# Gate and up projections of a SwiGLU layer: seven half-size products in place of eight, with the layer's input kept whole in DRAM

## The chip, the cores and the metric

The kernel runs on one core of one Trainium2 chip. The metric is device microseconds of the whole program, the median of three runs. Names used below: PE is TensorE (matmuls), PEld its weight loads, DVE VectorE, ACT ScalarE, POOL GpSimd, SP SyncE, whose queue issues most of the loads.

## The reference, cut to what matters

One layer of a diffusion trunk: a mixer (a gated delta rule in both directions beside a Fourier mixing), an output projection, and a SwiGLU feed-forward layer with a final norm. 2176 tokens (128 of a prompt, 2048 of a sample), 1024 channels, 2816 hidden columns. The change is in the feed-forward layer:

```
h2   = rmsnorm(x1, g_ffn) * (1 + scale2) + shift2      # x1: after the mixer's residual
g, u = split(h2 @ w_gu, 2)                             # [2176,1024] x [1024, 2*2816], float32
y    = x1 + gate2 * ((silu(g) * u) @ w_down)
out  = rmsnorm(y, g_final)
```

## The kernel before, in words

Activations lie transposed, channels on the partitions: 1024 channels are KT = 8 blocks of 128, and tokens run along the free axis. Float32 products are made of three matmuls: every operand is split into a high part (ACT, a copy that rounds to 12 bits) and a low part (DVE, the operand minus its high part), and PE adds high·high, high·low and low·high in PSUM. The high and low parts carry the letters h and l at the end of their names (wh, wl; ah, al; dh, dl).

The program has phases: the input projection, the inverses and the scans, then `outputs` (output projection and second norm of each tile of 128 tokens, beside the scans), then `phase_d`, the feed-forward layer, which starts near 1307 us of a span of 2889 us.

`out_norm` writes each tile's normalised input to DRAM in its two parts (`h2_d[0]` on ACT's queue, `h2_d[1]` on POOL's).

`phase_d` takes three blocks of tokens (768, 768 and 640), in the order in which `outputs` finishes their tiles, so the last tiles belong to the last block. For each block:

1. It loads the block's high and low parts (`h2`, L1173, on SP).
2. **Gate and up.** For each of FT = 22 column tiles j, and for gate then up: the weights of 128 columns, 1024 rows (`w_gu`, 512 KB, L1184, into the three slots of the pool "st"), are split into wh and wl (128x1024 each, two buffers each); for each half of the tokens (384 or 320) PE runs 8 k-blocks x 3 matmuls into one PSUM bank: 2 x 2 x 24 = 96 matmuls a tile. ACT puts Silu(gate) into `a`, DVE multiplies the up projection into it. All 22 `a` tiles stay in SBUF.
3. **Down.** For each half of the 1024 output columns: for each of the 22 k, split `a[k]` into ah, al and 512 weight columns (`w_dn`, L1222) into dh, dl, and run 3 matmuls for each tile of 128 tokens, into one bank a tile. Then for each tile the epilogue: `gy` = bank x gate2 (DVE), load of the residual from DRAM (`x_f`, L1246; two pieces in the second half), the sum (DVE), its squares (ACT). In half 0 the sum times g_final goes back to DRAM (L1252). In half 1 three small POOL instructions make `rstd`, ACT scales one piece and DVE the other, and POOL issues both writes of y (L1262).

`ah`, `al`, `dh`, `dl`, `gy` (6 buffers), `g2` (2) and `x_f` (4) have buffers of their own in the pool `dp`.

The order of instructions on each engine is not that of the code: a scheduler that simulates the engines sets it when the program is built, and each engine then runs its list in order. SP's list holds the loads of all steps, so a load that waits for a buffer holds back every later load. The helpers record all arithmetic at one line each (L117 matmul, L123 tensor_tensor, L133 activation).

Of the kernel before, what the change touches and what calls it, by code (L numbers as in the profile page):

```python
# [36 lines left out]

CONSTS = {}
# [47 lines left out]
class K:  # L86
# [51 lines left out]
    def split(self, hi, lo, src, eng=None, copy=None):  # L138
        """src = hi + lo, both with 12 significant bits."""
# [6 lines left out]
    def rsqrt(self, out, x):  # L146
        """out = x ** -0.5 for a few values per partition."""
# [25 lines left out]
    def psum(self, *banks):  # L173
        """PSUM's eight banks as rings of so many under the tags m, acc and tr."""
# [5 lines left out]
    def setup(self):  # L180
# [38 lines left out]
        self.h2_d = d([2, P, KT, N], F32, name="h2_d")  # L219
# [29 lines left out]
    def ada_tiles(self):  # L249
        """Places for a block of rows of w_ada in two parts and, for two blocks at a time, as it comes."""  # L250
# [6 lines left out]
    def mod_columns(self, which, *source):  # L257
        """The scale and shift of norm `which` (0: mix, 1: ffn) by channel: x -> x * a + b."""
# [7 lines left out]
    def load_split(self, hi, lo, src, width, raw_p, tag, *engs):  # L266
        """Rows of a weight (128 by width) into its two parts."""
# [4 lines left out]
    def norm(self, x, which, work):  # L272
        """rmsnorm of a tile of 128 tokens, and a place for its transpose."""
        h = work.tile([P, KT, P], F32, tag="h", name="h", bufs=2 - which)
# [7 lines left out]
    def norm_T(self, xn, h, which, r, hi, lo):  # L282
        """The transpose of a normalised tile, modulated, in two parts."""
        for g in range(2):
# [11 lines left out]
            ks = slice(g * 4, g * 4 + 4)  # L296
            self.split(hi[:, ks], lo[:, ks], h[:, ks])

# [44 lines left out]
    def phase_a(self, wk):  # L343
        """The normalised and modulated activations, transposed; the gates' inputs and f, by token."""
# [244 lines left out]
    def decays(self, work, c0, m):  # L589
        """exp of the difference of a chunk's cumulative decays, where it counts, for both pairs and directions."""  # L590
# [17 lines left out]
    def pair_products(self, work, n, c0, m, kq, dT, q, ssk):  # L608
        """For a pair of heads: decayed products of keys with keys and with queries; the keys by token."""
# [34 lines left out]
    def scales(self, work, c0, m, st, ssk):  # L644
        """Per token: strength / |k|^2 and strength / |k| (for the inverses), -decay / |k|."""
# [14 lines left out]
    def rows_of(self, pool, cols, dst):  # L660
        """The columns of `cols` to rows of DRAM."""
# [650 lines left out]
```

## Time and profile before

| | us |
|---|---|
| median of three runs (2886.11 to 2893.64) | 2887.48 |
| the profiled execution's span | 2888.6 |
| PE busy in it (95%) | 2731.7 |
| PEld busy (86%) | 2490.9 |
| DVE busy (51%) | 1470.7 |
| ACT busy (42%) | 1201.4 |
| POOL busy (12%) | 358.3 |

The profile is of one execution; its span is 1.1 us above the median. Busy time is the union of an engine's instructions; matmuls overlap one another, so the duration of one is longer than the distance to the next, and the rate is read from counts in a window or from the distance between starts. In a timeline row the bracket at the end says how long the engine stood idle before the instruction and what released it. PEclk is the granted clock as a share of full speed (1.00 is 2.4 GHz, half of it 1.2 GHz).

### The profile page before, as it was taken

The page shows a single profiled execution, that of the slowest core. Times are in us where ns is not written, and L with a number is a line of the kernel's source. Part 1 is how long each engine was busy: PE and PEld are TensorE (multiplying, and loading weights), DVE is VectorE, ACT ScalarE, POOL GpSimd, SP SyncE. Part 2 cuts the span into 40 slices and gives each one's busy share as a digit, 9 for nine tenths or more (in the row PEclk, how much of TensorE's full clock was granted, in tenths as well). Part 3 has the DMA queues.
Part 4 walks back from the last instruction along what each step waited for, and adds up shares of the span by engine and source line. Part 5 has one row for each costly group of instructions (what it writes and reads, how often), then busy time and mean ns, then how long its engine had stood idle before and what let it go on. Part 6 is the DMA issues. An engine that isn't in the chain of part 4 may idle for free.

```text
span 2888.6 us, 43615 instructions
## 1 busy us (share of the span) xinstructions
PE 2731.7 (95%) x16561; PEld 2490.9 (86%) x16561; DVE 1470.7 (51%) x2772; ACT 1201.4 (42%) x2587; POOL 358.3 (12%) x503
## 2 busy tenths in 40 slices
PE   7999788899899899998999999999999999999998
PEld 4888687788788778878999978899999789999986
DVE  6345698998997677762222225432222354222354
ACT  8755454332478778752111123321111333112243
POOL 1213244331200022210000000010000001000000
PEclk9999899899999999999999999999999999999999
DMA  9937775545456667674222243342122434322123
GB/s 322 293 121 210 194 219 168 162 154 184 138 179 200 197 198 221 214 211 147 66 60 65 66 128 115 101 139 66 59 66 65 118 110 158 93 79 74 59 94 133
DMA packets 440462, 407.54 MB, mean 141 GB/s; under 512 B 97932, under 2 KB 362556, under 8 KB 439356
## 3 DMA queue, kind: packets, MB, share of 16 engines
q1 hardware_dynamic: 349740, 308.77, 35.0%
q0 software_dynamic: 16384, 55.85, 5.7%
q10 hardware_dynamic: 74128, 40.13, 5.0%
q8 instruction: 131, 2.15, 0.3%
q14 instruction: 79, 0.65, 0.1%
HBM read 301.42 MB, written 103.25 MB: 140 GB/s over the span
## 4 chain that ended last, share of the span: by engine, by line
PE 38%; issue 13%; DMA 2%; SPq 1%; ACT 0%; DVE 0%; POOL 0%; POOLq 0%; ACTq 0%; DVEq 0%
PE m L117 19%; PE acc L117 19%; SPq L1173 1%; DMA x_f<-x_d 1%; DMA w_dn<-w_down 0%; DMA h_d<-h2h 0%; DMA h<-h_d 0%; DMA y<-x_f 0%; POOL rstd L123 0%; ACT gy L133 0%; DMA x_d<-x_f 0%; DVE x_f L123 0%; POOL rstd L127 0%; DVE gy L123 0%; ACT x_f L133 0%
## 5 line engine op out<-in xcount | busy, mean ns | idle before, releaser
L117 PE MATMUL acc<-h,wh 128*128 128x384 f32 (+1 forms) x2112 | 515.4, 327 | 2.3 <-DMA h<-h_d 2.3
L117 PE MATMUL m<-h,wh 128*128 128x384 f32 (+1 forms) x2112 | 512.4, 326 | 0.0
L133 ACT ACTIVATE wh<-w_gu 128x1024 fp32r<-128x1024 f32 x132 | 139.9, 1060 | 573.4 <-PE m L117 377.1
L117 PEld LDWEIGHTS acc<-h,wh 128*128 128x128 f32 x2112 | 373.9, 189 | 2.9 <-issue 2.6
L117 PEld LDWEIGHTS m<-h,wh 128*128 128x128 f32 x2112 | 371.9, 188 | 0.0
L123 DVE TENSOR_TENSOR wl<-w_gu,wh 128x1024 fp32r<-128x1024 f32 x132 | 161.7, 1225 | 396.1 <-ACT wh L133 396.1
L117 PE MATMUL acc<-hb,w_in 128*128 128x258 f32 (+1 forms) x2304 | 329.2, 299 | 19.2 <-DMA hb<-hT 13.7
L117 PE MATMUL acc<-h,wl 128*128 128x384 f32 (+1 forms) x1056 | 345.2, 327 | 0.4 <-DVE wl L123 0.4
L117 PE MATMUL m<-h,wl 128*128 128x384 f32 (+1 forms) x1056 | 344.1, 326 | 0.3 <-DVE wl L123 0.3
L117 PEld LDWEIGHTS acc<-hb,w_in 128*128 128x128 f32 x2304 | 314.0, 196 | 29.7 <-issue 13.1
L123 DVE TENSOR_TENSOR a<-a,m 128x384 f32<-128x384 f32 (+1 forms) x132 | 69.9, 531 | 347.1 <-PE m L117 347.1
L123 DVE TENSOR_TENSOR al<-a,ah 128x768 fp32r<-128x768 f32 (+1 forms) x128 | 117.2, 916 | 247.3 <-ACT ah L133 247.2
L133 ACT ACTIVATE ah<-a 128x768 fp32r<-128x768 f32 (+1 forms) x128 | 104.0, 813 | 301.3 <-PE acc L117 227.6
L117 PEld LDWEIGHTS acc<-h,wl 128*128 128x128 f32 x1056 | 199.2, 189 | 0.8 <-DVE wl L123 0.7
L117 PEld LDWEIGHTS m<-h,wl 128*128 128x128 f32 x1056 | 198.2, 188 | 0.6 <-DVE wl L123 0.6
L1252 POOL DMA_DIRECT2D x_d<-x_f x17 | 9.2, 541 | 1280.7 <-DVE x_f L123 1280.4
L117 PE MATMUL m<-dh,ah 128*128 128x512 f32 x384 | 151.2, 394 | 8.3 <-ACT dh L133 8.3
L117 PE MATMUL m<-dl,ah 128*128 128x512 f32 x384 | 150.2, 391 | 0.6 <-DVE dl L123 0.6
L117 PE MATMUL m<-dh,al 128*128 128x512 f32 x384 | 149.7, 390 | 0.0
L130 DVE SCALAR_TENSOR_TENSOR y<-conv_in,wconv,y 128x256 f32<-128x256 f32 (+1 forms) x216 | 126.2, 598 | 40.9 <-ACT conv_in L133 40.3
L133 ACT ACTIVATE a<-acc 128x384 f32<-128x384 f32 (+1 forms) x132 | 61.0, 463 | 191.7 <-PE acc L117 191.7
L117 PE MATMUL acc<-dh,ah 128*128 128x512 f32 x344 | 135.1, 393 | 0.0
(253 smaller groups left out, 5199.6 us busy)
## 6 DMA issues: line engine op xcount, KB each, us to landing
w_gu<-w_gu SPq DMA_DIRECT2D x132, 512.0 KB
pk<-pk_d SPq DMA_DIRECT2D x68, 512.0 KB
w_dn<-w_down SPq DMA_DIRECT2D x132, 256.0 KB
hb<-hT SPq DMA_DIRECT2D x104, 258.0 KB
h<-h_d SPq DMA_DIRECT2D x34, 512.0 KB
w_raw<-w_ada SPq DMA_DIRECT2D x32, 512.0 KB
x_f<-x_d SPq DMA_DIRECT2D x51, 256.0 KB
x<-x SPq DMA_DIRECT2D x17, 512.0 KB
```

The source lines that it names most:

```text
L117: self.nc.tensor.matmul(out, lhsT=lhsT, rhs=rhs, start=start, stop=stop)
L123: (eng or self.nc.vector).tensor_tensor(out=out, in0=a, in1=b, op=op)
L130: self.nc.vector.scalar_tensor_tensor(out=out, in0=a, scalar=s, in1=b, op0=op0, op1=op1)
L133: self.nc.scalar.activation(out=out, in_=in_, func=f, **kw)
L1173: nc.sync.dma_start(h2[i].bitcast(F32)[:, :, n * P:(n + 1) * P], self.h2_d[i, :, :, t * P:(t + 1) * P])
L1252: nc.gpsimd.dma_start(self.x1_d[rows, cols], x)
```

## The change

**Gate and up.** Channels, tokens and gate/up are each cut in halves (channels 0 to 511 and 512 to 1023; the block's first and second half of tokens; gate columns and up columns). The eight half-size products are replaced by Winograd's form of Strassen's seven. A product is now 4 k-blocks x 3 matmuls of the same shape as before, so a column tile takes 84 matmuls. The operands of the products are, beside the halves themselves, four sums of the weights' halves (S = u2+u1, S−g1, S3 = g1−u1, g2−S; 128x512 on DVE for each tile) and four sums of the inputs' halves (T1 to T4, once a block). Each product's weights are split on their own: 7 x (128x512 on ACT and on DVE) a tile in place of 2 x 128x1024; wh and wl have six buffers of 512 columns. Results: ACT copies the first product (V) and makes two Silus; seven DVE instructions of a half-block's width (384 or 320) add and multiply, where there were two. Three pairs of products accumulate in one bank, four banks a tile.

**Input.** `out_norm` writes h2 whole, once a tile; `norm`'s `h` has two buffers there. `ffn_inputs` loads, for each k-block, 128 x the block's tokens (eight loads, through the three slots of "st"), makes the sums (16 DVE instructions) and splits seven operands x 4 (28 on ACT, 28 on DVE).

**Buffers.** The down projection's tiles take the places of the inputs that the products no longer need: ah and al in those of h22, gy in those of T4, `x_f` in that of h21's high part, with three slots in place of four, and gate2 and g_final in that of h21's low part, with one slot for gate2. dh and dl share the six buffers of wh and wl.

```diff
-        h2h = wk.tile([P, KT, P], F32R, tag="h2h", name="h2h", bufs=1)
-        h2l = wk.tile([P, KT, P], F32R, tag="h2l", name="h2l", bufs=1)
-        self.norm_T(xn, h, 1, int(t == 16), h2h, h2l)
-        nc.scalar.dma_start(self.h2_d[0, :, :, rows], h2h.bitcast(F32))
-        nc.gpsimd.dma_start(self.h2_d[1, :, :, rows], h2l.bitcast(F32))
+        self.norm_T(xn, h, 1, int(t == 16), None, None)
+        at = FFN_AT[t]
+        self.nc.scalar.dma_start(self.h2_d[:, :, at:at + P], h)
...
+    def ffn_inputs(self, off, sub):
+        names = ("h11", "T1", "T2", "T3", "h21", "h22", "T4")
+        out = {n: [self.hp.tile([P, 4, HM], F32R, tag=n + x, name="h2") for x in "hl"] for n in names}
+        for c in range(4):
+            r = []
+            for k in (c, c + 4):
+                t = self.st.tile([P, D], F32, tag="st", name="h2_raw")
+                nc.sync.dma_start(t[:, :2 * sub], self.h2_d[:, k, off:off + 2 * sub])
+                r.append(t)
...
+            put("h11", h11)
+            total("T1", s, h12, h11)
+            total("T2", s, h22, s)
+            total("T3", s3, h22, h12)
+            total("T4", s, h21, s)
+            put("h21", h21)
+            put("h22", h22)
...
+    def gate_up(self, j, h2, a, sub, tag):
...
+            for k in range(4):
+                ws = slice(k * P, (k + 1) * P)
+                for i, (w_, h_) in enumerate(((wh, hh), (wh, hl), (wl, hh))):
+                    nc.tensor.matmul(o, lhsT=w_[:, ws], rhs=h_[:, k, :sub], start=start and k == i == 0,
+                                     stop=k == 3 and i == 2, skip_group_check=not start)
...
+        o = product(x, g1, "h11")
+        self.act(v, o)
+        self.tt(s, u2, u1, ALU.add)
+        oq = product(q, s, "T1")
+        self.tt(s, s, g1, ALU.subtract)
+        o = product(y, s, "T2")
+        self.tt(v, v, o, ALU.add)
+        self.tt(s3, g1, u1, ALU.subtract)
+        o = product(z, s3, "T3")
+        self.tt(u, v, o, ALU.add)
+        self.tt(u, u, oq, ALU.add)
+        o = product(x, g2, "h21", start=False)
+        self.act(a1, o, AF.Silu)
+        self.tt(s, g2, s, ALU.subtract)
+        o = product(q, s, "h22", start=False)
+        self.tt(a2, v, o, ALU.add)
+        self.act(a2, a2, AF.Silu)
+        o = product(z, u2, "T4", start=False)
+        self.tt(v, v, o, ALU.add)
+        self.tt(a2, a2, u, ALU.mult)
+        self.tt(a1, a1, v, ALU.mult)
...
-            dp = self.pool(ctx, "ffn_d", 2, side="left")
+            wp = self.wp = self.pool(ctx, "ffn_w", 6, side="left")
...
+                ahs, als = room("ah", F32R, "h22h"), room("al", F32R, "h22l")
+                tmps = room("gy", F32, "T4h", "T4l")
+                xs_ = room("x_f", F32, "h21h")
...
-                                x = dp.tile([P, 512], F32, tag="x", name="x_f", bufs=4)
+                                x = xs_[nx % 3]
+                                nx += 1
```

How the built order moves at three places (x at the end of a row is a count of like rows that follow one another):

SP's list at the end of block 0's down projection, half 1, before; `w_dn` are weights of the down projection, `x_f` the residual's pieces, `w_gu` the next block's weights (that block's `h` loads, 12 of them, stand further ahead):

```order
L1222 DMA w_dn<-w_down 128x512 x13
L1184 DMA w_gu<-w_gu 128x8x128 x5
L1236 DMA g_21992<-gate_d 128x512
L1236 DMA g_22664<-gate_d 128x512
L1246 DMA x_f<-x_d 128x512 x3
L1184 DMA w_gu<-w_gu 128x8x128
L1246 DMA x_f<-x_d 128x512 x3
L1184 DMA w_gu<-w_gu 128x8x128
L1246 DMA x_f<-x_d 128x512 x3
L1184 DMA w_gu<-w_gu 128x8x128
L1246 DMA x_f<-x_d 128x512 x3
L1184 DMA w_gu<-w_gu 128x8x128 x36
```

The weights of the next block begin ahead of the residual's last twelve pieces and go on between them. After, where `h_raw` are the next block's inputs and `gf` with gate_d is gate2:

```order
L1300 DMA w_dn<-w_down 128x512 x9
L1174 DMA h_raw<-h_d 128x768 x5
L1314 DMA gf<-gate_d 128x512
L1325 DMA x_f<-x_d 128x512 x9
L1174 DMA h_raw<-h_d 128x768 x3
L1204 DMA w_gu<-w_gu 128x8x128 x44
```

Now nine pieces of the residual follow one another, and three of the eight inputs and every weight of the next block stand behind them.

PE's list at the same place, before (`dh`, `dl` are the down projection's weights, h_18781 and h_18782 the next block's input):

```order
L117 MATMUL acc<-dh,ah 128x512
L117 MATMUL acc<-h_18781,wh 128x384
L117 MATMUL acc<-h_18782,wh 128x384
L117 MATMUL m<-dl,ah 128x512
L117 MATMUL m<-dh,al 128x512
L117 MATMUL acc<-dl,ah 128x512
```

The next block's first matmuls stand among the down projection's last ones. After, where h_19125 and h_19126 are the two parts of the next block's h11:

```order
L123 MATMUL m<-dl,ah 128x512
L123 MATMUL m<-dh,al 128x512
L123 MATMUL acc<-dh,ah 128x512
L123 MATMUL acc<-dl,ah 128x512
L123 MATMUL acc<-dh,al 128x512
L1218 MATMUL acc<-h_19125,wh 128x384
L1218 MATMUL acc<-h_19126,wh 128x384
L1218 MATMUL acc<-h_19125,wl 128x384
```

Now they begin behind the last one.

DVE's list at the start of block 0, before; the row with `tr,mod_cols` is the last tile's modulation, `wl` the first low part of gate weights:

```order
L123 TENSOR_TENSOR x_c<-x_c,gx 128x512
L123 TENSOR_TENSOR h2l<-h,h2h 128x512 x2
L127 TENSOR_SCALAR h<-tr,mod_cols 128x128 x4
L123 TENSOR_TENSOR h2l<-h,h2h 128x512 x2
L123 TENSOR_TENSOR wl<-w_gu,wh 128x1024
L123 TENSOR_TENSOR a<-a,m 128x384 x2
```

One split of the last tile (x2) stands between its modulation and the first `wl`. After, with the first six of the 41 instructions of this width (sums and low parts) that stand between that modulation and the first `wl`:

```order
L133 TENSOR_SCALAR h<-tr,mod_cols 128x128 x4
L129 TENSOR_TENSOR S<-h_raw 128x384
L129 TENSOR_TENSOR S_14694<-h_raw 128x384
L129 TENSOR_TENSOR S<-h_raw 128x384
L129 TENSOR_TENSOR h_14676<-h_raw,h_14675 128x384
L129 TENSOR_TENSOR h_14684<-h_raw,h_14683 128x384
L129 TENSOR_TENSOR h_14686<-h_raw,h_14685 128x384
```

The last tile's split is gone, and block 0's inputs are made there.

## Rows read from the trace of the kernel before

**Rows 1.** Busy time by stretch, in windows; the columns' names stand first.

```profile
core 0: us, PE busy (x) PEld busy (x) DVE busy (x) ACT busy (x) POOL busy (x), PEclk, DMA share, GB/s
1350.00:1400.00 50.00, 50.00 (x290) 50.00 (x289) 10.68 (x12) 8.98 (x12) 0.00 (x0) 1.00 0.22 64
1850.00:1900.00 50.00, 50.00 (x267) 47.05 (x266) 24.25 (x32) 19.57 (x34) 12.08 (x28) 1.00 0.59 184
2500.00:2550.00 50.00, 50.00 (x343) 50.00 (x342) 11.99 (x14) 10.14 (x14) 0.00 (x0) 1.00 0.26 78
```

**Rows 2.** Timeline of DVE, one column tile: start, duration, instruction, idle before.

```profile
1405.46 1.23 DVE L123 TENSOR_TENSOR wl<-w_gu,wh 128x1024 fp32r<-128x1024 f32 x1 [7.09 <-ACT wh L133]
...
1422.10 1.23 DVE L123 TENSOR_TENSOR wl<-w_gu,wh 128x1024 fp32r<-128x1024 f32 x1 [7.10 <-ACT wh L133]
```

**Rows 3.** Groups of DVE by shape, 1340 to 2890: busy, mean ns, idle.

```profile
L123 DVE TENSOR_TENSOR wl<-w_gu,wh 128x1024 fp32r<-128x1024 f32 x128 | 156.8, 1225 | 385.0 <-ACT wh L133 384.9
L123 DVE TENSOR_TENSOR dl<-w_dn,dh 128x512 fp32r<-128x512 f32 x128 | 87.5, 684 | 32.8 <-ACT dh L133 32.8
L123 DVE TENSOR_TENSOR a<-a,m 128x384 f32<-128x384 f32 x86 | 47.5, 553 | 246.8 <-PE m L117 246.8
```

**Rows 4.** Groups of ACT by shape, same stretch and columns.

```profile
L133 ACT ACTIVATE dh<-w_dn 128x512 fp32r<-128x512 f32 x128 | 78.8, 616 | 25.0 <-DMA w_dn<-w_down 25.0
L133 ACT ACTIVATE a<-acc 128x384 f32<-128x384 f32 x84 | 40.4, 481 | 136.5 <-PE acc L117 136.5
```

**Rows 5.** Timeline of DVE: epilogue of block 0, half 1.

```profile
1866.23 0.68 DVE L123 TENSOR_TENSOR gy<-acc,g 128x512 f32<-128x512 f32 x1
1866.82 0.68 DVE L123 TENSOR_TENSOR x_f<-x_f,gy 128x512 f32<-128x512 f32 x1
...
1880.17 0.69 DVE L123 TENSOR_TENSOR x_f<-x_f,gy 128x512 f32<-128x512 f32 x1 [2.73 <-DMA x_f<-x_d]
...
1887.86 1.22 DVE L123 TENSOR_TENSOR wl<-w_gu,wh 128x1024 fp32r<-128x1024 f32 x1
1888.99 0.95 DVE L123 TENSOR_TENSOR al<-a,ah 128x768 fp32r<-128x768 f32 x1
1892.79 0.69 DVE L123 TENSOR_TENSOR x_f<-x_f,gy 128x512 f32<-128x512 f32 x1 [2.85 <-DMA x_f<-x_d]
```

**Rows 6.** Timeline, POOL then SP's DMA queue: same tile as 1880.17.

```profile
1883.87 1.16 POOL L1262 DMA_DIRECT2D y<-x_f  x2 [1.05 <-ACT x_f L133]
1886.30 3.28 SPq L1246 DMA_DIRECT2D x_f<-x_d  x2
```

**Rows 7.** Timeline, SP then DVE: an x_f load in half 0.

```profile
1785.93 0.32 SPq L1246 DMA_DIRECT2D x_f<-x_d  x1
1788.60 0.69 DVE L123 TENSOR_TENSOR x_f<-x_f,gy 128x512 f32<-128x512 f32 x1 [0.63 <-DMA x_f<-x_d]
```

**Rows 8.** Timeline, SP then ACT: a weight load.

```profile
1852.74 0.38 SPq L1184 DMA_DIRECT2D w_gu<-w_gu  x1
1856.53 1.06 ACT L133 ACTIVATE wh<-w_gu 128x1024 fp32r<-128x1024 f32 x1 [0.81 <-DMA w_gu<-w_gu]
```

**Rows 9.** Timeline of PE: block 0, first down matmuls.

```profile
1705.45 0.80 PE L117 MATMUL m<-dh,ah 128*128 128x512 f32 x1 [5.95 <-ACT dh L133]
1706.05 0.63 PE L117 MATMUL acc<-dh,ah 128*128 128x512 f32 x1
1706.48 0.63 PE L117 MATMUL m<-dh,ah 128*128 128x512 f32 x1
```

**Rows 10.** Waits of PE, 1230 to 2890: us in all, times, longest.

```profile
PE m L117 <- ACT dh L133: 8.3, 2, 5.9
```

**Rows 11.** Timeline, PE then ACT: last tokens, start of block 0.

```profile
1307.34 0.99 PE L117 MATMUL acc<-h,wh 128*128 128x384 f32 x2
1307.79 1.57 ACT L133 ACTIVATE h<-tr,mod_cols 128x128 f32<-128x128 f32 x4 [1.51 <-PE tr L120]
```

**Rows 12.** DMA issues of the span: KB each, median us to landing.

```profile
h_d<-h2l POOLq DMA_DIRECT2D x17, 512.0 KB, 5.7
```

More of the change, by code (lines that the diff above doesn't have):

```diff
@@ L36 @@
 ORDER = [0, 7, 1, 6, 2, 5, 3, 4]
+BLOCKS = [[16, 8, 7, 9, 6, 10], [5, 11, 4, 12, 3, 13], [2, 14, 1, 15, 0]]
+FFN_AT = {t: n * P for n, t in enumerate(sum(BLOCKS, []))}
+M = 6 * P
+HM = M // 2
 CONSTS = {}
@@ L272, in norm @@
     def norm(self, x, which, work):
-        h = work.tile([P, KT, P], F32, tag="h", name="h", bufs=2 - which)
+        h = work.tile([P, KT, P], F32, tag="h", name="h")
         rstd = self.rstd(x, h.rearrange("p k t -> p (k t)"))
@@ L1153, in mixed, with put, total @@
         return make
+    def ffn_inputs(self, off, sub):
+        nc = self.nc
+        names = ("h11", "T1", "T2", "T3", "h21", "h22", "T4")
[6 more added lines that the diff above has]
+                r.append(t)
+            h11, h12 = r[0][:, :sub], r[0][:, sub:2 * sub]
+            h21, h22 = r[1][:, :sub], r[1][:, sub:2 * sub]
+            def put(name, src):
+                hi, lo = out[name]
+                self.split(hi[:, c, :sub], lo[:, c, :sub], src)
+            def total(name, t, a, b):
+                self.tt(t, a, b, ALU.subtract)
+                put(name, t)
+            s, s3 = (self.tp.tile([P, 512], F32, tag=n, name=n)[:, :sub] for n in ("S", "S3"))
+            put("h11", h11)
[5 more added lines that the diff above has]
+            put("h22", h22)
+        return out
@@ new lines, in gate_up, with product @@
+    def gate_up(self, j, h2, a, sub, tag):
+        nc, A = self.nc, self.A
+        raws = []
+        for part in range(2):
+            col = part * DFF + j * P
+            raw = self.st.tile([P, KT, P], F32, tag="st", name="w_gu")
+            nc.sync.dma_start(raw, A["w_gu"][:, col:col + P].rearrange("(k p) c -> p k c", p=P))
+            flat = raw.rearrange("p k c -> p (k c)")
+            raws.extend((flat[:, :512], flat[:, 512:]))
+        g1, g2, u1, u2 = raws
+        def product(ps, w, name, start=True):
+            wh = self.wp.tile([P, 512], F32R, tag="wh", name="wh")
+            wl = self.wp.tile([P, 512], F32R, tag="wl", name="wl")
+            self.split(wh, wl, w)
+            hh, hl = h2[name]
+            o = ps[:, :sub]
+            for k in range(4):
[3 more added lines that the diff above has]
+                                     stop=k == 3 and i == 2, skip_group_check=not start)
+            return o
+        x, y, z, q = (self.bank(tag) for _ in range(4))
+        v, u = (self.tp.tile([P, HM], F32, tag=n, name=n)[:, :sub] for n in "VU")
+        a1, a2 = a[:, :sub], a[:, sub:2 * sub]
+        s, s3 = (self.tp.tile([P, 512], F32, tag=n, name=n) for n in ("S", "S3"))
+        o = product(x, g1, "h11")
[19 more added lines that the diff above has]
+        self.tt(a1, a1, v, ALU.mult)
@@ L1165, in phase_d @@
+            self.hp = self.pool(ctx, "ffn_h", side="left")
+            self.tp = self.pool(ctx, "ffn_t", 2, side="left")
             up = self.pool(ctx, "ffn_a", side="left")
-            gf = None
-            for blk in blocks:
+            off = 0
+            for blk in BLOCKS:
                 m = len(blk) * P
                 sub = m // 2
-                h2 = [one.tile([P, KT, M], F32R, tag=f"h{i}", name="h2") for i in range(2)]
-                for i in range(2):
-                    for n, t in enumerate(blk):
-                        nc.sync.dma_start(h2[i].bitcast(F32)[:, :, n * P:(n + 1) * P],
-                                          self.h2_d[i, :, :, t * P:(t + 1) * P])
-                if gf is None:
-                    gf = one.tile([P, D], F32, name="gf")
-                    nc.sync.dma_start(gf, A["g_final"].partition_broadcast(P))
+                end = blk is BLOCKS[-1]
+                h2 = self.ffn_inputs(off, sub)
+                off += m
@@ L1200, in phase_d, with room @@
-                    acts.append(a)
+                    self.gate_up(j, h2, a, sub, "m" if j % 2 else "acc")
+                    acts.append(a)
+                def room(name, dtype, *parts):
+                    out = []
+                    for x in parts:
+                        t = self.hp.tile([P, 4, HM], dtype, tag=x, name=name).rearrange("p k t -> p (k t)")
+                        w = M if name in ("ah", "al") else 512
+                        out.extend(t[:, i * w:(i + 1) * w] for i in range(4 * HM // w))
+                    return out
@@ L1201, in phase_d @@
                 ss = self.small.tile([P, 2, 6], F32, tag="ssf", name="ssf", bufs=1)
+                nx = 0
                 for half in range(2):
@@ L1204, in phase_d @@
                     pss = [self.bank("acc" if n % 2 else "m") for n in range(len(blk))]
[L1205 removed]
+                    last = 4 if half and end else 0
                     ends = []
                     for k in range(FT):
[L1208 to L1219 removed]
+                        i = k - FT + last
+                        ah, al = (ehs[i], els[i]) if i >= 0 else (ahs[k % 2], als[k % 2])
+                        wh = wp.tile([P, 512], F32R, tag="wh", name="dh")
+                        wl = wp.tile([P, 512], F32R, tag="wl", name="dl")
                         self.split(ah[:, :m], al[:, :m], acts[k][:, :m])
```

66 lines of the change are left out of this document (17 added, 49 removed).

## The prediction

> **What bounds the kernel now.** I read the windows first, to find which engine fills the stretch that the change rewrites. In gate and up PE is busy for all of every window, at full granted clock (2.4 GHz), while DVE is busy for 11 to 12 us of 50 and ACT for 9 to 10 [rows 1]. So matmuls set the end of that stretch, and a matmul taken away is time gained for as long as nothing else comes late. The counts give the rate: 50 us / 290 = 172.4 ns for 384 columns, 50 / 343 = 145.8 ns for 320. A column tile of 96 matmuls takes 16.64 us, which the distance between the first splits of two tiles confirms [rows 2]. Then I read the stretch in which a block ends and the next begins, since there the order changes most: PE is busy for 50 of 50 us there too, though DVE, ACT, POOL and the DMA all have a good deal to do [rows 1]. Before, the residual's loads, the norm and the writes of y are hidden under the next block's matmuls, whose weights are loaded in between. Third, PE's list of waits: behind 1230 us the longest is 5.9 us, at the first down matmul of block 0, 8.3 us with that of block 1 [rows 10].
>
> **Gate and up: matmuls removed.** 84 matmuls of the same shape in place of 96: 12 x 172.4 = 2.07 us a tile for 44 tiles (two blocks) and 12 x 145.8 = 1.75 for 22: 91.0 + 38.5 = **-129.5 us**, all on the path if DVE and ACT keep up.
>
> Do they? A tile now wants from DVE seven low parts and four sums of 512, and seven instructions of 384. One alone lasts 0.68 and 0.55 us [rows 3], but those that follow one another start 0.59 us apart at 512 columns and 1.13 at 1024 [rows 5]; between these lies 0.46 for 384. 11 x 0.59 + 7 x 0.46 = 9.7 us of the 14.5 that PE now needs. With the whole durations it is 11 x 0.68 + 7 x 0.55 = 11.3. ACT wants 7 x 0.62 + 3 x 0.48 = 5.8 [rows 4]. In the built order splits stand five or six products ahead of PE, as the six buffers allow, and the next tile's first product is split ahead of this tile's last two, so a late low part has some 10 us of matmuls as its cover. I cost it at nothing. The pair of weight loads (3.8 us each from issue to use [rows 8]) finds its slot about 5 us ahead of need.
>
> **The two block ends (0 to 1, 1 to 2): a hole.** This decides the sum. In the new order PE goes from the last down matmul straight to the next block's first product, with nothing in between. That product needs its weights, which stand on SP's list behind nine residual loads and three input loads. The residual now has three slots at two pieces a tile. So from the second of six tiles on, each tile's second piece waits for the write of the first piece of the tile before to land, and its add waits for that load: five links in series, one behind another. In before they existed as well (four slots), but under matmuls.
>
> One link, from add to add: add to the issue of y 1880.17 to 1883.87 = 3.7 us (square, three POOL instructions, the scaling of the piece); from there to the waiting load's issue on SP 1886.30 = 2.4; from the load's issue to the next add, the second of the two issues being at 1886.30 + 3.28 - 0.32 = 1889.3, to 1892.79, 3.5, or in a quieter place 1785.93 to 1788.60 = 2.7 [rows 5 to 7]. The whole link measured there is 1880.17 to 1892.79 = 12.6, beside weight loads on the same DMA engines. In the hole those loads are absent (they wait behind), so I take the quiet pieces: 3.7 + 2.4 + 3.1 = 9.2, between 8.8 and 12.6.
>
> The Trainium skill ("DMA: Bandwidth & Descriptors", section "Anatomy of one DMA") gives about 2.0 us fixed plus bytes over 436 GB/s for GpSimd's transfers: an estimate of 2.6 for 256 KB, so 8.9 a link if it held for the load as well; by it the two holes would be 3 us shorter in all than by mine, and the trace's loaded 12.6 shows what it leaves out.
>
> The hole's terms: the first add falls about at PE's last matmul (-0.3); five links, 46; from the last add until both its writes of y have landed 3.7 + 2.4 + 0.6 for the second issue = 6.7. Then ACT, whose next split writes over the residual's slots and so waits for these writes, goes on: high part 0.5 and low part 0.5 free an input slot; the sixth input load 3.0; nine instructions of 384 on DVE up to the one that frees the slot for gate weights, 9 x 0.46 = 4.1; the weights 3.8; their high part 0.6: 12.5. Sum -0.3 + 46 + 6.7 + 12.5 = **65 us**. After such a pause PE restarts at half the clock (1.2 GHz): after its 5.95 us idle the matmuls start 0.43 apart in place of 0.23 [rows 9], ten or so, 2 us. So 67 a block end, **+134** for two; bounds 2 x 65 (link 8.8) and 2 x 84 (link 12.6).
>
> **Start of block 0.** Before, the first gate matmul starts at 1307.34, beside the last tile's modulation: that tile belongs to block 2, and block 0's inputs had been loaded in their two parts. Now 41 instructions of 384 stand on DVE between this modulation and the first low part of weights, and the weights' load stands behind eight input loads that share three slots. The second of the 41 writes where the last tile's `h` lay and so waits for that tile's write to DRAM. ACT's part of that modulation ends at 1307.79 + 1.57 = 1309.4 [rows 11], perhaps 1.5 earlier with the second buffer; the write lands about 5.7 later (median of the like writes [rows 12]); then 40 x 0.46 = 18.4, and some 2 of waits for loads that chase slots. 1309.4 - 1.5 + 5.7 + 18.4 + 2 = 1334.0, so **+26.7**; 16 if the write's wait is hidden and loads never stall, 34 if the write takes the loaded time and every slot is waited for.
>
> Here the skill speaks against the change ("VectorE: DVE Perf Modes", section "The TRN2 errata — SBUF-src ops pay a fixed extra latency per instruction"): many small instructions pay the fixed part each, and its formula for such adds gives an estimate of 0.557 us at 384 columns. The duration of one agrees (0.553 [rows 3]); the distances between starts do not pay all of it. By the page the 40 take 22.3, and the sum is 4 us higher.
>
> **The smaller parts.** First down matmuls: before, two waits of 8.3 in all plus some 2 us each of half clock, 12; now ah takes the place of h22, which the last product reads, so ACT's first split of 0.85 to 1.2 us stands on the path three times, with perhaps 1 us of slower clock each, 6.6: **-5.3**, between -12 and 0. `out_norm`: 34 ACT splits, 34 DVE splits and 17 writes fewer, where PE has only short waits: **-3**, between -8 and +3. One slot for gate2 and three for the residual in half 0 lie under the 18 matmuls a k-step there: nothing.
>
> **The sum,** made against the profiled span: 2888.6 - 129.5 + 134 + 26.7 - 5.3 - 3 = 2911.5. That span lies 1.1 us above the median of the runs, so I predict **2910.4 us**: the products' gain is paid back, and a little more, at the three places where a block's inputs are made.
>
> **The rivals.** *The holes are short, and the kernel is faster.* With the other terms as they are, two holes must stay below 111 in all to break even, so 53.5 each without the slow clock; five links then last 34.6, 6.9 each. The 3.7 on the engines is fixed by rows 5 and 6, so write and load would have to take 3.2 together where the shortest rows give 2.4 and 2.7. For it: in the hole the DMA engines are all but idle, a state in which no row here shows this pair. Against it: both shortest rows already come from places with gaps. Links of 6.2 would give 2888 - 15 - 1 = about 2873. Chance of a time under 2878.8: 0.13.
>
> *Loaded links.* The links last 12.6 as in before: +34, 2944. Against it the weight loads are missing. Chance of 2930 to 2960: 0.15.
>
> *Gate and up starve.* ACT's high part and DVE's low part alternate seven times a tile. If no low part overlapped anything, DVE would need 9.7 + 7 x 0.62 = 14.0, just under 14.5; with the whole durations, 11.3 + 4.3 = 15.6, 1.1 over, and at 66 tiles each us a tile costs 66: 2910 + 73 = 2983. From 14.5 us a tile it decides. Against it stands the built order with its six buffers. Chance 0.08.
>
> *The change does not do what it says:* the built order could keep another matmul rate, such as a loss at each of seven ends of a product in place of four. 0.2 us x 3 x 66 = 40 us, 2950. The before's ends of a product show no such loss in a full window [rows 1]. Chance 0.02, in the slower cases.
>
> **How the numbers follow.** My forecast, 2888 to 2930 with the most likely at 2910, has 0.62; of that 0.15 falls within 0.3% of before (8.7 us, about what a measurement of this kernel can tell from no change), where links of 8.8 and a start of 16 to 20 meet. Range: the low end takes in links of 6.9 with a short start, 2880; the high end the loaded links with the long start, 2910 + 34 + 7 = 2951, rounded up to 2956 for the smaller parts. About 0.1 lies on either side. Faster 0.13; same 0.15; slower 0.72.
>
> **What would show it.** Gate and up windows with 290 and 343 matmuls in 50 us, PE busy for all of it, and 14.5 us between like splits of two tiles: the first term. Two idle stretches of PE of some 65 us with SP's loads of `x_f` waiting for writes of y five times in a row: the second; if PE is idle there for under 53, the sum turns. PE's first gate matmul near 1334. I am wrong if matmuls in gate and up wait for wl or wh more than once in a while, or if the links overlap in some way that the order doesn't show.

## The result and the profile after

The changed kernel takes 2911.03 us (median, 2908.87 to 2911.95), the kernel before 2887.59 beside it: a ratio of 1.0068, interval 1.0051 to 1.0084. It is 23.4 us slower, where 2910.4 had been forecast. The profiled execution has a span of 2908.8 us, 20.2 above that of before.

PE in the page's forty slices of the span:

```profile
PE   6999798899899899977999999299999991999998
```

Behind the middle a 2 and a 1 stand out, where before had nothing under 8: the two block ends. The two 7s ahead of them hold the start of block 0. Everywhere else in the feed-forward layer PE is as full as it was. Two windows of gate and up (stretch, its length, PE busy and count, PEld, DVE, ACT, POOL, granted clock, DMA share, GB/s):

```profile
1350.00:1400.00 50.00, 50.00 (x291) 50.00 (x290) 36.80 (x65) 19.12 (x34) 0.00 (x0) 1.00 0.26 74
2500.00:2550.00 50.00, 50.00 (x343) 50.00 (x342) 39.66 (x74) 20.95 (x40) 0.00 (x0) 1.00 0.30 85
```

These answer to [rows 1]: 291 and 343 matmuls in 50 us, where there were 290 and 343, at the full clock. A tile of 84 therefore takes 14.5 us. DVE's share has gone from 11 or 12 us of 50 to 37 or 40, and PE does not wait for it.

PE's three long pauses in its timeline, the last transposes of the output projection ahead of them (start, duration, instruction, idle before):

```profile
1298.62 1.73 PE L126 MATMUL tr<-const_all,xn 128*128 128x128 f32 x8 [4.71 <-ACT xn L139]
...
1327.62 0.69 PE L1218 MATMUL acc<-h,wh 128*128 128x384 f32 x1 [27.27 <-ACT wh L139]
...
1897.53 0.69 PE L1218 MATMUL acc<-h,wh 128*128 128x384 f32 x1 [64.55 <-ACT wh L139]
...
2467.12 0.90 PE L1218 MATMUL acc<-h,wh 128*128 128x320 f32 x2 [65.14 <-ACT wh L139]
```

And PE's waits from 1230 us on (in all, times, longest):

```profile
PE acc L1218 <- ACT wh L139: 157.0, 3, 65.1
PE m L123 <- ACT ah L139: 7.2, 4, 4.0
```

157.0 us in three waits for the first weights of a block. From the rows: the matmuls give -129.5. Block 0 starts at 1327.62 in place of 1307.34 [rows 11], +20.3, the 27.27 us of idle less the 7 by which the output projection ends earlier. The two holes give 64.55 + 65.14 = +129.7. The first down matmuls wait for 7.2 where 8.3 was waited [rows 10], -1.1 in idle time alone. The sum is 19.4 of the 20.2. Not in it are the slow matmuls behind the three pauses, 2.7 us each (last section), and, against them, what before lost in its own places: 2.3 us of waiting for `h` early in block 0, slow matmuls behind that and behind the waits of [rows 10], and 10.1 us behind its last matmul, where it is 8.7 now. These nearly cancel.

**The five links.** DVE's timeline in the first hole, the six additions of the residual:

```profile
1831.93 0.69 DVE L129 TENSOR_TENSOR x_f<-x_f,gy 128x512 f32<-128x512 f32 x1
...
1841.19 0.69 DVE L129 TENSOR_TENSOR x_f<-x_f,gy 128x512 f32<-128x512 f32 x1 [1.72 <-DMA x_f<-x_d]
...
1850.21 0.69 DVE L129 TENSOR_TENSOR x_f<-x_f,gy 128x512 f32<-128x512 f32 x1 [5.59 <-DMA x_f<-x_d]
...
1858.99 0.69 DVE L129 TENSOR_TENSOR x_f<-x_f,gy 128x512 f32<-128x512 f32 x1 [5.36 <-DMA x_f<-x_d]
...
1867.64 0.69 DVE L129 TENSOR_TENSOR x_f<-x_f,gy 128x512 f32<-128x512 f32 x1 [5.22 <-DMA x_f<-x_d]
...
1876.14 0.69 DVE L129 TENSOR_TENSOR x_f<-x_f,gy 128x512 f32<-128x512 f32 x1 [5.07 <-DMA x_f<-x_d]
```

The distances are 9.26, 9.02, 8.78, 8.65 and 8.50: 8.84 a link, the low bound of the forecast (8.8 to 12.6, 9.2 taken). GpSimd's queue shows the write of y between the second and the third:

```profile
1844.88 1.16 POOL L1341 DMA_DIRECT2D y<-x_f  x2 [1.05 <-ACT x_f L139]
```

From the addition at 1841.19 to the write 3.7 us, as in before; from the write to the next addition 5.3 for landing and load, where 2.4 + 3.1 had been put. SP's nine loads in that stretch form one group, and the next loads stand behind it:

```profile
1838.59 35.53 SPq L1325 DMA_DIRECT2D x_f<-x_d  x9
1885.06 4.80 SPq L1174 DMA_DIRECT2D h_raw<-h_d  x3
1892.87 6.25 SPq L1204 DMA_DIRECT2D w_gu<-w_gu  x3
```

SP's waits between 1828 and 1892 us name the cause (in all, times, longest):

```profile
SPq L1325 <- DMA y<-x_f: 38.5, 9, 7.8
```

The DMA engines' share in the hole is the last but one number of this window, their GB/s the last:

```profile
1833.00:1876.00 43.00, 0.00 (x0) 0.00 (x0) 10.54 (x16) 8.77 (x19) 10.43 (x25) 0.52 0.35 122
```

That is little more than a link's own four transfers (two writes and two loads of 256 KB in 8.84 us are 119 GB/s); before had 0.59 and 184 in the like stretch [rows 1].

Before did not have these five links. Its six additions start at 1866.82, 1868.62, 1880.17, 1884.51, 1892.79 and 1896.64; the two that [rows 5] leaves out:

```profile
1884.51 0.69 DVE L123 TENSOR_TENSOR x_f<-x_f,gy 128x512 f32<-128x512 f32 x1 [0.91 <-DMA x_f<-x_d]
...
1896.64 0.69 DVE L123 TENSOR_TENSOR x_f<-x_f,gy 128x512 f32<-128x512 f32 x1 [0.43 <-DMA x_f<-x_d]
```

With four slots at two pieces a tile, a tile's loads wait for the writes of the tile before the last one, so there are two chains side by side, of two links each. The 12.6 from 1880.17 to 1892.79 is the step from a tile to the next but one, and it ends with the second piece: the write issued at 1884.49, the load that it released at 1889.26, the addition 3.5 later. The six additions span 29.8 us in before and 44.2 here, although the DMA engines were busier in before: the slot that is gone costs more than the quiet brings. With four slots and links of 8.84, two in series would take some 18 us in place of 44 (an estimate; no run has four slots and nothing else changed).

ACT goes on only behind the last writes of y, and then the inputs are finished:

```profile
1883.92 0.94 ACT L139 ACTIVATE h<-h_raw 128x384 fp32r<-128x384 f32 x2 [3.21 <-DMA y<-x_f]
...
1896.85 0.63 ACT L139 ACTIVATE wh<-w_gu 128x512 fp32r<-128x512 f32 x1 [1.16 <-DMA w_gu<-w_gu]
```

So the hole's terms measure -1.1 (first addition against PE's last matmul), 44.2 (five links), 7.8 (last addition to 1883.92) and 13.6 (from there to the first product): 64.55, where -0.3, 46, 6.7 and 12.5 had been put.

### The profile page after: what moved, and what is told of

The parts are those of the page before. It is cut to its first block, busy times and chain, and to the rows that moved or that the text cites. A ratio compares the mean times of both kernels' runs of the same rounds, so it can differ in the third digit from the quotient of the medians.

```text
span 2908.8 us, 43847 instructions
## 1 busy us (share of the span) xinstructions
PE 2608.4 (90%) x15769; PEld 2368.8 (81%) x15769; DVE 1958.5 (67%) x3794; ACT 1396.2 (48%) x3033; POOL 341.6 (12%) x486
## 4 chain that ended last, share of the span: by engine, by line
PE 55%; DMA 4%; DVE 2%; ACT 2%; issue 1%; POOL 1%; ACTq 0%; POOLq 0%; SPq 0%; DVEq 0%
PE acc L1218 16%; PE m L1218 16%; PE acc L123 12%; PE m L123 11%; DMA y<-x_f 1%; DMA x_f<-x_d 1%; DMA z_s<-z_d 1%; DMA h_raw<-h_d 1%; PE tr L126 1%; POOL rstd L129 1%; DMA w_gu<-w_gu 0%; DVE x_f L129 0%; ACT gy L139 0%; ACT h L139 0%; DVE h L129 0%
## 5 line engine op out<-in xcount | busy, mean ns | idle before, releaser
L1218 PE MATMUL acc<-h,wh 128*128 128x384 f32 (+1 forms) x1848 | 453.8, 330 | 157.0 <-ACT wh L139 157.0
L1218 PEld LDWEIGHTS acc<-h,wh 128*128 128x128 f32 x1848 | 330.3, 191 | 158.2 <-ACT wh L139 158.2
L1218 PE MATMUL m<-h,wh 128*128 128x384 f32 (+1 forms) x1848 | 448.0, 326 | 1.1 <-DVE U L129 1.1
L139 ACT ACTIVATE wh<-S 128x512 fp32r<-128x512 f32 x264 | 163.6, 631 | 350.3 <-DVE S L129 163.5
L1218 PEld LDWEIGHTS m<-h,wh 128*128 128x128 f32 x1848 | 325.1, 188 | 1.4 <-ACT a L139 1.4
L1218 PE MATMUL acc<-h,wl 128*128 128x384 f32 (+1 forms) x924 | 302.1, 330 | 0.0
L1218 PE MATMUL m<-h,wl 128*128 128x384 f32 (+1 forms) x924 | 299.4, 326 | 0.4 <-DVE wl L129 0.4
L129 DVE TENSOR_TENSOR wl<-S,wh 128x512 fp32r<-128x512 f32 x264 | 179.0, 687 | 16.7 <-ACT wh L139 15.9
L139 ACT ACTIVATE wh<-w_gu 128x512 fp32r<-128x512 f32 x198 | 123.8, 629 | 122.7 <-PE m L1218 44.7
L129 DVE TENSOR_TENSOR wl<-w_gu,wh 128x512 fp32r<-128x512 f32 x198 | 135.3, 685 | 16.2 <-ACT wh L139 16.0
```

Source lines behind the costliest of these rows:

```text
L129: (eng or self.nc.vector).tensor_tensor(out=out, in0=a, in1=b, op=op)
L139: self.nc.scalar.activation(out=out, in_=in_, func=f, **kw)
L1218: nc.tensor.matmul(o, lhsT=w_[:, ws], rhs=h_[:, k, :sub], start=start and k == i == 0, stop=k == 3 and i == 2, skip_group_check=not start)
```

## The experiments

All ratios are to the kernel before, run on the same chip in the same job; its medians there were 2892.0 for the fewer matmuls, the residual, the whole epilogue and the start of block 0; 2893.1 for the two banks; 2890.6 for the sums on GpSimd; and 2893.2 for the last three.

**Fewer matmuls in the kernel before.** Is a removed matmul worth its whole time?

```diff
-  self.mm(o, wl[:, k], h2[0][:, k, ss], start=False, stop=(k == KT - 1))
+  if k % 3 != 0:
+      self.mm(o, wl[:, k], h2[0][:, k, ss], start=False, stop=(k == KT - 1))
```

> The kernel before, with 84 matmuls a column tile in place of 96 and nothing else changed: low weights by high inputs is left out for three of the eight channel blocks (so the output is only nearly the reference's). If matmuls alone set gate and up, 44 x 12 x 172.4 ns + 22 x 12 x 145.8 ns = 129.5 us go: 2758, between 2755 and 2762. The rival, that part of a removed matmul was hidden anyway, gives less: a gain of 100 or under.

2762.75 us, ratio 0.9558 (0.9543 to 0.9573): 129.2 us less than its companion runs, where 129.5 had been expected (the time itself lies 0.75 above the range, which had been counted from 2887.5). The whole of a removed matmul is on the path, and the change's gain is real; it is spent elsewhere.

**The residual out of the ring.**

```diff
-                            if last:
+                            if half:
                                 x = up.tile([P, M], F32, tag="a", name="x_f", bufs=FT)[:, :512]
```

> The changed kernel, with the residual's pieces of half 1 in the places of `a` tiles that are done with (as the last block has them already), so that no load of x_f waits for a write of y; gate2 and g_final stay where they are. If the five links in series make the hole, 5 x 8.8 = 44 us of each go and what is left is the epilogue on the engines (gate2's slot is held until its last instruction, some 12 us) and the inputs' tail of some 12: holes of 22 to 28, and a time of 2911 - 2 x 40 = 2831, between 2820 and 2840. If the making of the inputs sets the hole, the links being beside it, under 10 us each go: 2890 or more.

2839.68 us, ratio 0.9829 (0.9812 to 0.9847): some 70 us less than the changed kernel, and faster than before by 1.7%. The hole is halved:

```profile
1861.92 1.01 PE L1218 MATMUL acc<-h,wh 128*128 128x384 f32 x2 [33.67 <-ACT wh L139]
```

33.7 in place of 64.55, and at the second block end 31.0 in place of 65.14. So 30.9 and 34.2 us went with the links, about half of each hole, where 44 had been expected: what is left is 6 to 12 longer than the 22 to 28 expected in the first hole. DVE's timeline shows why:

```profile
1835.29 2.49 DVE L129 TENSOR_TENSOR x_f<-x_f,gy 128x512 f32<-128x512 f32 x4
...
1846.09 1.41 DVE L136 SCALAR_TENSOR_TENSOR x_f<-x_f,rstd,gf 128x512 f32<-128x512 f32 x2 [2.10 <-POOL rstd L129]
1847.53 1.03 DVE L129 TENSOR_TENSOR h<-h_raw,h 128x384 fp32r<-128x384 f32 x2
1852.87 0.56 DVE L129 TENSOR_TENSOR S<-h_raw,S 128x384 f32<-128x384 f32 x1 [4.31 <-DMA h_raw<-h_d]
```

The additions now follow one another, but the last scalings wait for `rstd` until 1846.09 and hold the place of h21's low part; then comes the sixth input load, 4.3 of waiting in the row of 1852.87, since its slot came free only with that low part.

**The whole epilogue out of the inputs' places.** On top of the last one (v1), g_final, gate2 and gy of half 1 lie among the `a` tiles, and h22 is split by `rest`, called behind the loads of a block's first weights. This run is called v2 below:

```diff
+                    gfh = up.tile([P, M], F32, tag="a", name="gf", bufs=FT)[:, :512]
...
+                                g2 = up.tile([P, M], F32, tag="a", name="g2", bufs=FT)[:, :512]
...
-                        tmp = tmps[n]
+                        tmp = up.tile([P, M], F32, tag="a", name="gy", bufs=FT)[:, :512] if half else tmps[n]
...
-            put("h22", h22)
+        def rest():
+            for c in (0, 2):
+                t = self.st.tile([P, D], F32, tag="st", name="h22_raw")[:, :2 * sub].rearrange("p (k t) -> p k t", k=2)
...
```

> As the one before, and gate2, g_final and gy of half 1 lie in places of `a` too, and h22 is split from loads of its own that come after the first weights: of the next block's inputs only h22 waits for the end of the down projection. If the rest of the hole is the wait for the epilogue's places, it is gone and 2 to 5 us stay at each block end: 2911 - 2 x 62 = 2787, between 2780 and 2795. If the rest is the vector and scalar engines' load there (12 additions, 12 squares, rstd, and 44 + 28 splits), holes of 10 to 20 stay: 2800 to 2820.

2802.3 us, ratio 0.9701 (0.9683 to 0.972). The hole of 33.7 is gone; PE starts the next block with no pause, and then stops for shorter ones, 10.0 us in all at this block end. The two longest:

```profile
1835.43 0.71 PE L1226 MATMUL acc<-h,wh 128*128 128x384 f32 x2 [3.63 <-DVE gy L129]
...
1852.50 0.98 PE L1226 MATMUL acc<-h,wh 128*128 128x384 f32 x2 [5.29 <-ACT h L139]
```

The first waits for a PSUM bank that the epilogue still reads, the second for the high part of h22, the input that is loaded last. The time lies at the low end of the second theory's 2800 to 2820: the places and the late h22, which this run changes together, were most of the rest, and the vector engine, busy for 26 of 30 us there, is the next candidate:

```profile
1820.00:1850.00 30.00, 22.47 (x103) 19.51 (x101) 26.37 (x47) 15.23 (x33) 10.69 (x18) 0.93 0.71 232
```

**Two banks of each ring.** Is that wait of 3.6 us for a bank on the path?

```diff
-        x, y, z, q = (self.bank(tag) for _ in range(4))
+        x, q, y, z = (self.bank(t) for t in ("m", "acc", "m", "acc"))
```

> As v2, with a column tile's four banks taken two and two from the rings m and acc in place of all four from one, so that the first two products of a block find the two banks that the down projection doesn't hold. In v2's profile the second product waits 3.6 us and a later one 0.5 for the gate2 multiplication that frees a bank, at each block end. If that wait is on the path, 3 to 4 us a block end go: 2802 - 7 = 2795, a ratio to before near 0.967 where v2's was 0.970. If another wait (the low parts, h22) ends as late, nothing moves.

2804.9 us, ratio 0.9702 (0.9687 to 0.9717): nothing moved against v2, whose edit it contains. The wait for the bank is gone, and others stand in its place:

```profile
1840.15 0.62 PE L1226 MATMUL m<-h,wh 128*128 128x384 f32 x2 [1.14 <-ACT wh L139]
...
1844.22 0.69 PE L1226 MATMUL m<-h,wl 128*128 128x384 f32 x1 [2.41 <-DVE wl L129]
```

The wait for h22 behind them has shrunk to 3.1. That wait stood at the first block end alone; at the second, the longest is for a bank that the addition into U still reads, 4.4 us in v2 and 5.3 here. DVE is at 27 of 30 us at the first block end:

```profile
1820.00:1850.00 30.00, 24.34 (x105) 20.54 (x104) 27.09 (x48) 14.83 (x30) 9.02 (x12) 0.89 0.65 207
```

**The sums on GpSimd.** Then is the vector engine's load what is left?

```diff
-                self.tt(t, a, b, ALU.subtract)
+                self.tt(t, a, b, ALU.subtract, eng=nc.gpsimd)
```

> As v2, with the 16 sums of a block's inputs (T1 to T4) on GpSimd in place of the vector engine. If the vector engine's load sets what is left of the block ends (27 of 30 us busy there in v2) and the start of block 0, 16 x 0.46 = 7.4 us leave it at each of three places: 10 to 20 us less than v2's 2802, 2782 to 2792. If the scalar engine's high parts, the loads or the slower sums themselves come as late, nothing is won: 2798 to 2810.

2807.37 us, ratio 0.9698 (0.9668 to 0.9729): nothing won. One such sum lasts 1.3 us there, 2.8 times the vector engine's distance of 0.47 (group of GpSimd, busy and mean ns):

```profile
L129 POOL TENSOR_TENSOR S<-h_raw,S 128x384 f32<-128x384 f32 x16 | 21.0, 1319 | 10.5 <-DVE h L129 8.2 <-DMA h_raw<-h_d 2.4
```

And the vector engine was not relieved. In the window in which v2 has it busy for 26.37 us with 47 instructions, 38 take it 28.15:

```profile
1820.00:1850.00 30.00, 21.90 (x97) 18.28 (x96) 28.15 (x38) 14.88 (x28) 12.68 (x13) 0.94 0.57 187
```

The reason stands in the timelines of DVE and of GpSimd:

```profile
1829.36 1.37 DVE L129 TENSOR_TENSOR h<-S,h 128x384 fp32r<-128x384 f32 x1
1830.65 1.35 DVE L129 TENSOR_TENSOR h<-h_raw,h 128x384 fp32r<-128x384 f32 x1
1831.92 0.55 DVE L129 TENSOR_TENSOR h<-S,h 128x384 fp32r<-128x384 f32 x1
...
1829.05 2.54 POOL L129 TENSOR_TENSOR S<-h_raw 128x384 f32<-128x384 f32 x2 [0.49 <-DVE h L129]
```

While GpSimd makes its sums, until 1831.6, a subtraction of the vector engine lasts 1.36 us in place of 0.55. Over the layer the 34 input instructions of this width that overlap a sum last 1.07 us in the mean, the other 22 last 0.55. So the run moved work off the vector engine without making it less busy, and whether its load sets the rest of the block ends stays open.

**The start of block 0: loads or arithmetic?**

```diff
-                t = self.st.tile([P, D], F32, tag="st", name="h2_raw")
+                if off == 0:
+                    t = self.up.tile([P, M], F32, tag="a", name="h2_raw", bufs=FT)
+                else:
+                    t = self.st.tile([P, D], F32, tag="st", name="h2_raw")
...
```

> The changed kernel, with block 0's eight input loads into the still empty places of `a` in place of the three slots, so that no load of inputs waits for a split and the weights' loads pass them. Two theories of the 27.3 us that PE stands idle at the start of block 0. If the 41 vector instructions set it, as the prediction had it, they still take 19 us behind the last write's landing, and 2 to 4 us go: 2907 to 2909. If the loads that chase three slots, and the weights behind them, set it, 10 us or more go: 2901 or less.

2911.15 us, ratio 1.0075 (1.0053 to 1.0097): no gain, and above the range of either theory. PE's timeline there:

```profile
1303.71 1.73 PE L126 MATMUL tr<-const_all,xn 128*128 128x128 f32 x8 [4.71 <-ACT xn L139]
1308.29 0.69 PE L1221 MATMUL acc<-h,wh 128*128 128x384 f32 x1 [2.84 <-ACT h L139]
1315.40 0.69 PE L1221 MATMUL acc<-h,wh 128*128 128x384 f32 x1 [6.42 <-DVE h L129]
...
1335.94 1.01 PE L1221 MATMUL acc<-h,wh 128*128 128x384 f32 x2 [15.32 <-ACT wh L139]
```

The loads no longer hold anything up, and the first product runs from 1315 on; but the second waits 15.3 us for its weights, whose sum the vector engine makes behind most of the other operands. 24.6 us of idle are left of 27.3. That did not shorten the start: from the last transposes to block 0's first down matmul it is 354.7 us here and 353.6 in the changed kernel, because PE also runs the first product, and again the matmuls behind the 15.3, at the lower clock (granted 0.50 from 1315.4 to 1318.8 and from 1335.9 to 1339). The vector engine, too, gets going later: it waits 6.7 us for ACT until 1313.4, 9.7 behind the last transposes, where it was 7.1 in the changed kernel. So early loads alone bring nothing; what the instructions alone would take is not shown by this run.

**Each input just ahead of its product.** On top of v2, block 0's inputs made one operand after another:

```diff
         def product(ps, w, name, start=True):
+            if j == 0 and "make" in h2:
+                h2["make"](name)
...
```

> As v2, and block 0's inputs are made one operand after another, each just ahead of its product, from raw inputs that lie where `a` will lie; its first weights are loaded ahead of them. If the start of block 0 is set by the 41 instructions because all of them stand ahead of the first product, PE now starts some 12 us earlier and loses part of that again by waiting for T2 and T3, since the vector engine needs about 27 us for the inputs and the first tile where PE needs 14.5: 8 to 12 us less than v2, 2790 to 2794. If the sum of that engine's work alone sets it, whatever its order, under 4 us go: 2798 or more.

2805.03 us, ratio 0.9694 (0.968 to 0.9709): 2 us at most against v2's ratio, within the second theory's range. The time alone does not decide, though: from the last transposes to block 0's first down matmul it is 347.1 us here and 352.1 in v2, 5 us gained, and the output projection ends 5.3 us later in this profile (1302.05 against 1296.73), which hides them. While PE works and waits in turn, DVE is busy for all of the 20 us:

```profile
1320.00:1340.00 20.00, 14.70 (x59) 13.35 (x60) 19.97 (x40) 8.95 (x19) 0.00 (x0) 0.74 0.18 52
```

The scheduler also put the splits of h21 and h22, whose inputs were there, ahead of T2. The order that the code asks for is not the order that runs, and what the asked one would bring is not shown.

**Two buffers for the weights.** The cover on which the forecast laid the splits' cost:

```diff
-            wp = self.wp = self.pool(ctx, "ffn_w", 6, side="left")
+            wp = self.wp = self.pool(ctx, "ffn_w", 2, side="left")
```

> The changed kernel with two buffers of wh and wl in place of six. If throughput alone decides (9.7 us of vector work for 14.5 of matmuls), under 5 us are lost: 2911 to 2916. If the splits' lead over PE is the cover, as the prediction had it, two or more of the seven products of a tile wait, since the additions and multiplications of a tile stand between its splits: 0.3 to 1 us a tile, 20 to 66 us in all, 2931 to 2977.

2966.62 us, ratio 1.0258 (1.0242 to 1.0273): 55 us slower than the changed kernel. PE runs 271 matmuls in a window where it ran 291:

```profile
1350.00:1400.00 50.00, 47.88 (x271) 46.48 (x270) 35.56 (x60) 18.59 (x33) 0.00 (x0) 1.00 0.23 64
```

The waits for a low part are short and many:

```profile
PE acc L1218 <- DVE wl L129: 12.7, 27, 1.3
PE m L1218 <- DVE wl L129: 9.4, 22, 0.8
```

They make up 22 us. From its first product to its first down matmul, with all small delays, each block takes longer: 338.6, 340.0 and 300.8 us in place of 324.6, 324.6 and 280.3, 50 us of the 55. DVE is busy for 36 us of 50, no more than with six buffers. So throughput is not enough: the lead is what keeps PE from waiting.

**What out_norm no longer does.** Put back, with one buffer of h again and the low part written to a place nobody reads:

```diff
-        self.norm_T(xn, h, 1, int(t == 16), None, None)
+        wk, rows = self.wk, slice(t * P, (t + 1) * P)
...
+        self.norm_T(xn, h, 1, int(t == 16), h2h, h2l)
+        self.nc.gpsimd.dma_start(self.h2l_d[:, :, rows], h2l.bitcast(F32))
```

> The changed kernel, whose output norm also does again what it did before: one buffer of h, 17 tiles split into two parts (34 splits on each of two engines), and the low part written to DRAM by the queue of GpSimd, to a place that nobody reads. If these are the 7 us by which the output projection ends earlier in the profile after (1298.6 against 1305.7 at its last transposes), they come back: 2915 to 2919, its last transposes near 1305. If that difference is how the scans happened to run, nothing moves by more than 3 us: 2908 to 2914.

2921.78 us, ratio 1.0101 (1.0081 to 1.0121) against 1.0068: some 9.5 us, with intervals that overlap a little, and a time above the 2915 to 2919 expected. Its last transposes come 14.7 us later than the changed kernel's 1298.62, not 7, and PE waits longer for the last tile's norm, 9.32 us in place of 4.71:

```profile
1313.32 1.97 PE L126 MATMUL tr<-const_all,xn 128*128 128x128 f32 x8 [9.32 <-ACT xn L139]
```

In the eight profiles of kernels with the changed `out_norm` the last transposes lie between 1294.4 and 1303.7, in the three with the old work (before, the one with fewer matmuls, and this one) at 1305.7, 1312.9 and 1313.3. The two groups do not overlap, so the splits and writes cost time in this phase. How much stays uncertain: single profiles of the two groups differ by 2 to 19 us.

## Why the prediction was right

*The matmuls removed*, -129.5: 129.2 measured alone, and windows with the same count in the changed kernel.

*Gate and up at no further cost*: right, and for the reason given. The cover is the lead of six buffers; with two it is gone and 55 us are lost, 50 of them in gate and up.

*The block ends*, +134: measured 129.7 of idle and 2.7 of slow matmuls behind each pause, 135 in all. The one disputed term, the link, was 8.84 against 9.2: with the DMA engines busy for 0.35 of the time, write and load took what their shortest rows had given, not less and not the loaded figure. Other sums inside the hole were off by about 1 us each and nearly cancelled. The estimate of 8.9 a link from the Trainium skill's figures ("DMA: Bandwidth & Descriptors", section "Anatomy of one DMA") agrees with the 8.84 of the hole. That the links fill 44.2 of 64.55 us is read from the timeline; taking them away won 30.9 and 34.2, about half of each hole, since the epilogue's other places came next.

Three things in the prediction's text were wrong without moving its number. Before did not have the five links under its matmuls: with four slots it had two chains of two, and its 12.6 spans two tiles, so the high bound rested on a link of another kind. The rival with links of 6.2 gives 2910.4 - 10 x 3.0 = 2880 by the prediction's own terms, not 2873, so it would have been within 0.3% of before. And the low bound for the start of block 0, 16, is not what its terms give: 26.7 - 5.7 - 2 = 19.

*The start of block 0*, +26.7, and *out_norm*, -3: together 23.7, where 20.3 was measured (27.3 of idle, the phase ahead 7 earlier). PE's start was put at 1334.0 and came at 1327.62. ACT's timeline, the last tile's write and the first weights:

```profile
1302.05 0.52 ACTq L1113 DMA_DIRECT2D h_d<-h  x1
...
1326.94 0.63 ACT L139 ACTIVATE wh<-w_gu 128x512 fp32r<-128x512 f32 x1 [1.45 <-DMA w_gu<-w_gu]
```

DVE's, the instruction that waits for the write and the last one of this width ahead of the weights:

```profile
1305.71 1.03 DVE L129 TENSOR_TENSOR S<-h_raw 128x384 f32<-128x384 f32 x2 [4.12 <-DMA h_d<-h]
...
1325.79 0.55 DVE L129 TENSOR_TENSOR h<-S,h 128x384 fp32r<-128x384 f32 x1
```

And SP's loads:

```profile
1307.23 11.64 SPq L1174 DMA_DIRECT2D h_raw<-h_d  x5
1323.13 6.07 SPq L1204 DMA_DIRECT2D w_gu<-w_gu  x3
```

The write is issued at 1302.05 where 1307.9 had been put: -5.9, the output projection's earlier end, so out_norm's -3 was too small for this profile; since that end moves by up to 9 us between profiles of kernels with the same `out_norm`, how well it was hit is partly luck. It lands 3.7 later, not 5.7: -2.0. From there to 1325.79 it is 20.1 where 18.4 + 2 had been put. The weights, issued at 1323.13 behind the inputs, are used at 1326.94, and 1.8 from 1325.79 to 1327.62 had not been in the sum. -5.9 - 2.0 - 0.3 + 1.8 = -6.4. That the instructions and not the slots fill this time is read from the timeline: of the 20.1 us DVE stands idle for 1.3. The run with block 0's inputs in other places fits this (2.7 us less idle), but it changed the order of ACT too. The Trainium skill's formula ("VectorE: DVE Perf Modes", section "The TRN2 errata — SBUF-src ops pay a fixed extra latency per instruction") gives an estimate of 0.557 us, which agrees with the duration of one, 0.55; but those that follow one another start 0.47 apart (1322.04, 1322.51 and 1322.98 in this stretch), and the 22.3 for the forty was not seen.

*The first down matmuls*, -5.3 against -1.1: mis-sized. The waits for ah are 7.2 us in four, the longest 4.0, where three of 0.85 to 1.2 had been put. (The -5.3 also holds slower clock on both sides; of idle time alone some -4.7 had been put.)

The start came 3.4 lower than forecast and the first down matmuls 4.2 higher, and they nearly cancel, so the agreement to 1 us is better than the terms deserve; each lay within its bounds.

## What to carry to other kernels

Saving matmuls pays in full where PE is the bound, but not before the operands' making has a place that overlaps with the work before it: here 130 us were gained in the steady part and 150 lost at three seams. When buffers are shared to make room, follow who must let go of them, through the DMA queues as well: a ring of three slots at two pieces a tile turned a hidden epilogue into five round trips of 9 us, where four slots had made two chains of two, and held back every weight behind it on the same queue. Memory whose content is already dead (here the activations' tiles in the second half) was there for the asking, and using it turned a loss of 0.7% into a gain of 3%.

## What the runs showed of the hardware

The link's DMA pair, a 256 KB write of y and the 256 KB load that waits for it, took 5.3 us with the DMA engines busy for 0.35 of the time, mostly by these transfers, and 4.8 + 3.5 = 8.3 beside weight loads in before (write issued at 1884.49, load at 1889.26, addition at 1892.79 [rows 5, 6]). A subtraction of 128x384 float32 lasts 0.55 us on the vector engine, 0.47 from start to start, and 1.3 on GpSimd with the vector engine at work beside it (0.99 for the one that ran alone, at 1304.7 in the run with the sums on GpSimd). The vector engine's own last up to 1.37 while such a sum runs. After the pause of 64.55 us PE's first eighteen matmuls of 384 columns start 0.32 us apart, at the lower of the two clocks (1.2 GHz; granted 0.50 from 1897.5 to 1900.5), in place of 0.172:

```profile
1901.30 0.52 PE L1218 MATMUL acc<-h,wl 128*128 128x384 f32 x1
1901.62 0.84 PE L1218 MATMUL acc<-h,wh 128*128 128x384 f32 x2
```

That costs 2.7 us; behind the 27 us at the start of block 0 it is the same number of slow matmuls, so the longer pause cost no more on restarting.
